# Layer 0 attention of a two-layer diffusion backbone: score tiles kept in PSUM, a bank for the context outputs, half heads ended later, dense bias tables

## The chip, the cores and the metric

The kernel runs on one core of one Trainium2 chip. The metric is device time in microseconds: the median over the runs of one kernel. All arithmetic is on fp32 data; each matmul operand is split into a high part in the matmul's own format (fp32r) and a low rest, so that most products take three matmuls (high x high, high x low, low x high).

## The reference, cut to what matters

1024 latent tokens on a 16 x 64 grid and 256 context tokens, width 1024, go through two layers. Layer 0 mixes by 16 heads of 64: eight neighbourhood heads (0 to 7), each query over a window of 8 rows by 16 columns and over the context, and eight grouped-query heads (8 to 15) over all 1280 tokens.

```python
# neighbourhood head: bias per (row offset, column offset), window scores and context scores in one softmax
col_bias = rpb[:, :, col_idx - cols[:, None] + (WIN_C - 1)]
s_win = einsum('bhqd,bhrqjd->bhrqj', q_r, k_win) * scale + bias
s_ctx = einsum('bhqd,bhkd->bhqk', q_r, kc) * scale
p = softmax(concatenate([s_win, s_ctx]))
# context tokens attend among themselves, in all 16 heads
yc_na, yc_g = grouped_attention(cnq, cnk, cnv), grouped_attention(cgq, cgk, cgv)
# six modulation vectors a layer
m = silu(cond) @ ada_w[l] + ada_b[l]
```

Then come the output projection, a SwiGLU layer, and layer 1 with differential attention, which the change leaves alone.

## The kernel before

All loads, and nearly all stores, are issued from SyncE's queue (SPq in the profile). The program is written in an order of its own and a scheduler of the framework places the instructions on the engines' queues by priority; within one tag the tiles of a pool go round a fixed number of buffers in the program's order. `later()` lowers the priority of what is written inside it by 3000, `tc.high_priority` raises it.

**Projections of layer 0** (to some 405 us). The value projection goes in two groups `g`, then chunks `ch` 0 to 7 give the neighbourhood heads' queries (0 to 3) and keys (4 to 7). Four things are slipped in between:

- `ada_acc` loads a modulation weight in eight tiles of 512 KB (tag `aw`, 3 buffers) and accumulates them on VectorE for two conditions (L210, L214); `ada_sum` adds the columns up with 16 small matmuls for each condition (L235) into a PSUM tile of tag `q`, 3 buffers here. Modulation 2 is loaded before the value projection, 3 at group 1, 4 at chunk 1, all under `later()`; the sums stand at group 1, chunk 1 and chunk 4.
- `tables(i, h)` builds the bias tables of a pair of heads for both orientations: a row of 15 x 127 values is broadcast into 64 partitions (L630), the column mask is added on GpSimd (L631) and the result is stored to DRAM (L634), in two tiles of tag `aw` with four loads and four stores in all. There are eight such calls, two in each value group and one in each of chunks 0 to 3. `skew` later reads each row at its own offset, so that row c of a table is shifted by c: 64 values at a time.
- `early` runs the first steps of `maxima`: for each head a score matmul without the split (L432) into a `q` tile and a row maximum on VectorE (L410; L406 with the bias). The largest value of each query is later taken off the scores by a 65th row of the key operand. 200 steps are asked for by the end of chunk 7, `EARLY0`; the rest (`side0`) run beside attention, done before head `NEWH` = 2.
- The operands of the first heads are loaded.

**Attention of layer 0** (474 to 913 us), heads 8 to 15, then 0 to 7. A head has one unit of the context tokens among themselves (256 queries, two key chunks side by side) and two halves of 512 queries: 10 key chunks each for a grouped-query head (21 units), 2 context chunks and 5 window units for a neighbourhood head (15 units). A unit is: two matmuls into a score tile `pst` (L853, L854); for a window unit the bias added by VectorE into an SBUF tile `sb` (L877); the exponential on ScalarE into `sb` (L843); the high part `hi`, on VectorE in one unit of three and on ScalarE otherwise (L846, L848); the low part `lo` = e - hi, on VectorE in one of four and on GpSimd otherwise (L849). Some units later three matmuls with the values follow (`pv_one`, L888 to L891), `LAG0` = 5 units behind, `LAGN` = 7 from head 2 on, where the flag `wide` is set. `finish` ends a half: logarithm and exponential of the sums (L901, L902) and three VectorE instructions (L903 to L905).

PSUM has eight banks: 3 `t` for scores, 3 `q` for maxima (from head 2 on also for every second score tile), 2 `v` for the outputs. At the end of each head all pending products run:

```python
            while pend:
                pv_one()
```

Of the kernel before, what the change touches and what calls it, by code (L numbers as in the profile page):

```python
# [9 lines left out]
F32 = mybir.dt.float32  # L10
# [7 lines left out]
P = 128  # L18
# [8 lines left out]
RPW = 127  # L27
RPN = 15 * RPW
# [4 lines left out]
LEADP, EARLY0, VSHARE, HIDVE, LAG0, PLHN = 0.9, 200, 0.3, 3, 5, 2  # L33
QB, VB, TB, X0, LOD = 3, 2, 3, 9, 4
# [18 lines left out]
def kernel(ctx: ExitStack, tc: tile.TileContext, xT, cond, ada_w, ada_b, win0, wv0, wout0, rp, rpf, qg, kg,  # L53
# [5 lines left out]
    def nm(s):  # L59
        uid[0] += 1  # L60
        return f"{s}_{uid[0]}"
# [55 lines left out]
    def dram(shape, name):  # L117
        return dpool.tile(shape, F32, name=name)
# [13 lines left out]
    sk = [dram([8, 64 * RPN + 2048], f"sk{i}") for i in range(2)]  # L132
# [18 lines left out]
    def skew(i, h, dr0, n):  # L151
        o = 63 + dr0 * RPW
        v = sk[i][h, o : o + 64 * (RPN - 1)].rearrange("(c n) -> c n", c=64)
        return v[:, : n * RPW].rearrange("c (u y) -> c u y", y=RPW)[:, :, :GW]

# [3 lines left out]
    def ps(tag, bufs, w=512):  # L159
        return pq[0].tile([P, w], F32, tag=tag, bufs=bufs, name=nm("ps" + tag))  # L160
# [137 lines left out]
    def later():  # L298

        return tc.high_priority(-LATER)  # L300
# [184 lines left out]
    with sbuf("hp0", 8) as hp, sbuf("a10", 8) as ap:  # L485
# [134 lines left out]
        cmt = ap.tile([P, 2, RPW], F32, tag="cmt", bufs=1, name="cmt")  # L620

        def tables(i, h):

            for d0, d1 in ((0, 8), (8, 15)):
                n = d1 - d0
                T = ap.tile([P, 8, RPW], F32, tag="aw", bufs=3, name=nm("sk"))[:, 0:n, :]
                T2 = T.rearrange("p u y -> p (u y)")
                for j in range(2):
                    src = (rpf, rp)[i][h + j : h + j + 1, d0 * RPW : d1 * RPW].to_broadcast([64, n * RPW])
                    nc.sync.dma_start(T2[64 * j : 64 * j + 64], src)  # L630
                nc.gpsimd.tensor_add(T, T, cmt[:, i : i + 1, :].to_broadcast([P, n, RPW]))  # L631
                for j in range(2):
                    dst = sk[i][h + j, : 64 * RPN].rearrange("(c n) -> c n", c=64)[:, d0 * RPW : d1 * RPW]
                    nc.sync.dma_start(dst, T2[64 * j : 64 * j + 64])  # L634

# [79 lines left out]
        for ch in range(8):  # L715
# [13 lines left out]
            if ch in (1, 4):  # L729
                ada_sum(*pend_ada, qmt)  # L730
            if ch == 1:
                with later():
                    pend_ada = ada_acc(ap, *adas.pop(0))
# [7 lines left out]
    with sbuf("a20") as ap, psum("pa20") as pq[0]:  # L741
# [4 lines left out]
        def stt_():  # L746

            turn[0] += 1
            return qmt() if wide and turn[0] % 2 else ps("t", TB)
# [106 lines left out]
        def attend(h):  # L856
# [11 lines left out]
            def unit(o, pieces, b=None):  # L868
# [3 lines left out]
                e = half()[:, :tot]  # L872
# [7 lines left out]
                hi, lo = probs(pst[:, :tot] if pieces[0][4] is None else e, tot, e)  # L880
# [4 lines left out]
            def pv_one():  # L885
# [6 lines left out]
                if done:  # L892
                    done()
# [14 lines left out]
            unit(pvt(), [(kc, 0, 256, 0, None) for kc in range(2)], 0)  # L908
# [12 lines left out]
            while pend:  # L921
                pv_one()

        pend = []
# [547 lines left out]
```

## Time and profile before

| | us |
|---|---|
| median of 3 runs | 3656.18 (3655.86 to 3661.64) |
| profiled execution, its time | 3658.97 |
| its span in the profile | 3657.2 |
| TensorE busy | 3415.5 (93%) |
| VectorE busy | 2218.4 (61%) |
| ScalarE busy | 1422.3 (39%) |
| GpSimd busy | 825.2 (23%) |

The span is the profiled execution from its first to its last instruction. Busy times are modelled for matmuls: each is shown until its result is out, so two in a row overlap, and the distance of their starts says what one costs.

### The profile page before, as it was taken

The numbers are of one execution on the slowest core, as the hardware profiler recorded it, in microseconds if no ns is written. First come the engines' busy times: TensorE is split into PE (matmuls) and PEld (weight loads), VectorE is DVE, ScalarE is ACT, GpSimd is POOL, SyncE is SP. The second block draws the span as 40 slices with busy tenths as digits, with TensorE's granted clock in tenths as the row PEclk, the third lists the DMA queues.
The fourth block names the chain that finished last, engine by engine and source line by source line (L and its number), as shares of the span: only waits on it lengthen the run. The fifth ranks groups of instructions, "written<-read, shape, count | busy, mean of one in ns | idle before, by whom it ended". The sixth has DMA issues, their size and how long they took to land.

```text
span 3657.2 us, 43706 instructions
## 1 busy us (share of the span) xinstructions
PE 3415.5 (93%) x16044; PEld 2783.9 (76%) x16044; DVE 2218.4 (61%) x3555; ACT 1422.3 (39%) x2862; POOL 825.2 (23%) x622
## 2 busy tenths in 40 slices
PE   6799699988999999999998899899999999999997
PEld 4588577766888888888886678787666888888886
DVE  7767388887755555554336366787998533433335
ACT  4431067666441111111115254797777421111112
POOL 3212177766220000000003322002332200000002
PEclk8899789999999999999999999999999999999999
DMA  5276764374413333231112553646442211111111
GB/s 212 78 241 223 219 136 103 87 142 97 165 52 98 104 104 98 93 98 47 35 41 87 135 140 100 201 149 189 125 127 91 98 47 50 49 53 47 47 47 64
DMA packets 198081, 394.51 MB, mean 108 GB/s; under 512 B 57692, under 2 KB 99216, under 8 KB 197866
## 3 DMA queue, kind: packets, MB, share of 16 engines
q1 hardware_dynamic: 196074, 388.62, 36.0%
q0 software_dynamic: 1792, 3.10, 0.2%
q8 instruction: 126, 2.06, 0.2%
q14 instruction: 89, 0.73, 0.1%
HBM read 317.03 MB, written 74.61 MB: 107 GB/s over the span
## 4 chain that ended last, share of the span: by engine, by line
PE 74%; DVE 10%; ACT 5%; POOL 3%; issue 3%; DMA 3%; SPq 1%; POOLq 0%; DVEq 0%; ACTq 0%
PE psd L181 6%; PE psd L182 6%; PE psd L183 6%; PE psg L181 5%; PE psg L182 5%; PE psg L183 5%; PE psu L183 4%; PE psu L181 4%; PE psu L182 4%; PE psm L183 4%; PE psm L182 4%; PE psm L181 4%; PE pst L1318 2%; PE psq L1063 2%; PE pst L1319 2%
## 5 line engine op out<-in xcount | busy, mean ns | idle before, releaser
L173 POOL TENSOR_TENSOR wl<-wr,wh 128x1024 fp32r<-128x1024 f32 x69 | 168.0, 2435 | 1521.7 <-ACT wh L172 1315.4
L172 ACT CAST wh<-wr 128x1024 fp32r<-128x1024 f32 x193 | 202.2, 1049 | 761.7 <-PE psd L182 305.7
L993 DVE SCALAR_TENSOR_TENSOR x<-psd,mods,x 128x512 f32<-128x512 f32 (+1 forms) x448 | 301.3, 686 | 190.7 <-PE psd L183 190.4
L1027 DVE TENSOR_TENSOR sg<-sg,psu 128x512 f32<-128x512 f32 (+1 forms) x110 | 69.6, 634 | 484.4 <-PE psu L183 477.9
L181 PE MATMUL psd<-ah,wh 128*128 128x512 f32 (+1 forms) x896 | 331.3, 370 | 8.8 <-DVE x L993 6.8
L182 PE MATMUL psd<-al,wh 128*128 128x512 f32 (+1 forms) x896 | 328.3, 366 | 0.0
L183 PE MATMUL psd<-ah,wl 128*128 128x512 f32 (+1 forms) x896 | 326.9, 366 | 0.8 <-DVE wl L173 0.7
L181 PE MATMUL psg<-hh,wh 128*128 128x512 f32 (+1 forms) x880 | 326.2, 371 | 0.9 <-ACT sg L1024 0.9
L183 PE MATMUL psg<-hh,wl 128*128 128x512 f32 (+1 forms) x880 | 325.3, 370 | 0.1
L182 PE MATMUL psg<-hl,wh 128*128 128x512 f32 (+1 forms) x880 | 325.0, 369 | 0.0
L183 PE MATMUL psu<-hh,wl 128*128 128x512 f32 (+1 forms) x880 | 323.8, 368 | 0.5 <-POOL wl L173 0.5
L181 PE MATMUL psu<-hh,wh 128*128 128x512 f32 (+1 forms) x880 | 324.1, 368 | 0.0
L182 PE MATMUL psu<-hl,wh 128*128 128x512 f32 (+1 forms) x880 | 323.6, 368 | 0.0
L173 DVE TENSOR_TENSOR wl<-wr,wh 128x1024 fp32r<-128x1024 f32 x124 | 156.0, 1258 | 220.7 <-ACT wh L172 204.8
L1065 DVE TENSOR_REDUCE st<-psq 128x1 f32<-128x512 f32 (+1 forms) x384 | 219.4, 596 | 58.3 <-PE psq L1064 53.5
L1066 ACT ACTIVATE psq<-psq,st 128x512 f32<-128x512 f32 (+1 forms) x384 | 226.8, 594 | 65.0 <-DVE st L1065 61.3
L181 PE MATMUL psm<-hh,wh 128*128 128x512 f32 (+1 forms) x584 | 219.2, 376 | 25.7 <-ACT wh L172 18.4
L849 POOL TENSOR_TENSOR pl<-sb,ph 128x512 fp32r<-128x512 f32 (+1 forms) x144 | 203.5, 1420 | 91.9 <-ACT ph L848 60.2
L182 PE MATMUL psm<-hl,wh 128*128 128x512 f32 (+1 forms) x584 | 217.4, 373 | 6.5 <-DVE hl L349 4.7
L183 PE MATMUL psm<-hh,wl 128*128 128x512 f32 (+1 forms) x584 | 217.9, 373 | 3.7 <-POOL wl L173 3.7
L181 PEld LDWEIGHTS psd<-ah,wh 128*128 128x128 f32 x896 | 169.4, 189 | 44.0 <-DVE x L993 13.5
L1024 ACT ACTIVATE sg<-psg 128x512 f32<-128x512 f32 (+1 forms) x110 | 60.5, 552 | 344.4 <-PE psg L183 344.4
(276 smaller groups left out, 8331.2 us busy)
## 6 DMA issues: line engine op xcount, KB each, us to landing
aw<-in_ada_w SPq DMA_DIRECT2D x112, 512.0 KB
wr<-in_wg SPq DMA_DIRECT2D x44, 512.0 KB
wr<-in_wu SPq DMA_DIRECT2D x44, 512.0 KB
wr<-in_wd SPq DMA_DIRECT2D x44, 512.0 KB
k<-ks SPq DMA_DIRECT2D x32, 640.0 KB
wr<-in_wout SPq DMA_DIRECT2D x32, 512.0 KB
q<-qs SPq DMA_DIRECT2D x32, 512.0 KB
k<-ks SPq DMA_DIRECT2D x48, 320.0 KB
```

The source lines that it names most:

```text
L172: nc.scalar.copy(hi, raw)
L173: (eng or nc.gpsimd).tensor_sub(lo, raw, f(hi))
L181: nc.tensor.matmul(o, ah, bh, start=start, stop=False)
L182: nc.tensor.matmul(o, ah, bl, start=False, stop=False)
L183: nc.tensor.matmul(o, al, bh, start=False, stop=stop)
L849: (nc.vector if npb[0] % LOD == 0 else nc.gpsimd).tensor_sub(lo, e, f(hi))
L993: nc.vector.scalar_tensor_tensor(xv, pst, mods[:, l, ci, 40 + oc : 41 + oc], xv, op0=ALU.mult, op1=ALU.add)
L1063: nc.tensor.matmul(p1, q2[:, a * P : a * P + P], k2[:, k0 : k0 + kw], start=True, stop=False)
L1065: nc.vector.tensor_reduce(st[:, 0, a, j : j + 1], p1, axis=AX.X, op=ALU.max, negate=True)
L1066: after_table(nc.scalar.activation(p1, p1, AF.Exp, bias=st[:, 0, a, j : j + 1], accum_out=st[:, 1, a, j : j + 1]))
L1318: nc.tensor.matmul(o, ks[c][1][:, kk], qs[c][1][:, c0 : c0 + 512], start=True, stop=False)
L1319: nc.tensor.matmul(o, ks[c][0][:, kk], qs[c][0][:, c0 : c0 + 512], start=False, stop=True)
```

## The change

Host side: the bias tables come as dense arrays `tabT` and `tabQ`, already laid out row by row with the shift of `skew` in them (64 columns in place of 127), gathered from the same values; the masks are 64 wide. `tables` is one tile, one load, one GpSimd addition and one store per call (16 DMAs in all for 64), and `skew` reads straight rows.

The last modulation accumulation (modulation 4) is written without `later()`, and its sum goes from chunk 4 to chunk 6.

In attention: `keep` marks the units whose low part VectorE makes: one of four as before, and every second one once `wide` is set. Their exponential (and the bias sum before it) is written in place into the PSUM score tile and not into `sb`. The high part is made on VectorE in one unit of four, never in a kept one. The context unit's output has a bank of its own (tag `c`), `q` has 2 buffers in place of 3, and of the wide heads' score tiles two of five take a `q` bank. `finish` is called two products (`LATEF`) after a half's last, and pending products are carried over from one head to the next.

```diff
-LEADP, EARLY0, VSHARE, HIDVE, LAG0, PLHN = 0.9, 200, 0.3, 3, 5, 2
-QB, VB, TB, X0, LOD = 3, 2, 3, 9, 4
+LEADP, EARLY0, VSHARE, LAG0, PLHN = 0.9, 200, 0.3, 5, 2
+QB, VB, TB, X0, LATEF = 2, 2, 3, 9, 2
...
     def skew(i, h, dr0, n):
-        o = 63 + dr0 * RPW
-        v = sk[i][h, o : o + 64 * (RPN - 1)].rearrange("(c n) -> c n", c=64)
-        return v[:, : n * RPW].rearrange("c (u y) -> c u y", y=RPW)[:, :, :GW]
+        return sk[i][64 * h : 64 * h + 64, dr0 * GW : (dr0 + n) * GW].rearrange("c (u y) -> c u y", y=GW)
...
         def tables(i, h):
-            for d0, d1 in ((0, 8), (8, 15)):
-                n = d1 - d0
-                T = ap.tile([P, 8, RPW], F32, tag="aw", bufs=3, name=nm("sk"))[:, 0:n, :]
-                T2 = T.rearrange("p u y -> p (u y)")
-                for j in range(2):
-                    src = (rpf, rp)[i][h + j : h + j + 1, d0 * RPW : d1 * RPW].to_broadcast([64, n * RPW])
-                    nc.sync.dma_start(T2[64 * j : 64 * j + 64], src)
-                nc.gpsimd.tensor_add(T, T, cmt[:, i : i + 1, :].to_broadcast([P, n, RPW]))
-                for j in range(2):
-                    dst = sk[i][h + j, : 64 * RPN].rearrange("(c n) -> c n", c=64)[:, d0 * RPW : d1 * RPW]
-                    nc.sync.dma_start(dst, T2[64 * j : 64 * j + 64])
+            T = ap.tile([P, 15, GW], F32, tag="aw", bufs=3, name=nm("sk"))
+            r = slice(64 * h, 64 * h + P)
+            nc.sync.dma_start(T.rearrange("p u y -> p (u y)"), (tabT, tabQ)[i][r])
+            nc.gpsimd.tensor_add(T, T, cmt[:, i : i + 1, :].to_broadcast([P, 15, GW]))
+            nc.sync.dma_start(sk[i][r], T.rearrange("p u y -> p (u y)"))
...
-            if ch in (1, 4):
+            if ch in (1, 6):
                 ada_sum(*pend_ada, qmt)
             if ch == 1:
-                with later():
-                    pend_ada = ada_acc(ap, *adas.pop(0))
+                pend_ada = ada_acc(ap, *adas.pop(0))
...
-            return qmt() if wide and turn[0] % 2 else ps("t", TB)
+            return qmt() if wide and turn[0] % 5 in (1, 3) else ps("t", TB)
...
-        def probs(src, w, e):
-            lo, hi = spare.pop() if spare else plh_more() if npb[0] % PLHN == 1 else plh()
+        def probs(src, w, e, keep):
+            lo, hi = spare.pop() if spare else plh_more() if npb[0] % PLHN == 0 else plh()
             lo, hi = lo[:, :w], hi[:, :w]
             after_table(nc.scalar.activation(e, src, AF.Exp))
-            npb[0] += 1
-            if npb[0] % HIDVE == 0:
+            if npb[0] % 4 == 2:
                 nc.vector.tensor_copy(hi, e)
             else:
                 nc.scalar.copy(hi, e)
-            (nc.vector if npb[0] % LOD == 0 else nc.gpsimd).tensor_sub(lo, e, f(hi))
+            (nc.vector if keep else nc.gpsimd).tensor_sub(lo, e, f(hi))
...
-                e = half()[:, :tot]
+                npb[0] += 1
+                keep = npb[0] % 2 == 1 if wide else npb[0] % 4 == 3
+                e = pst[:, :tot] if keep else half()[:, :tot]
...
                 if done:
-                    done()
+                    ends.append([LATEF, done])
+                for x in ends:
+                    x[0] -= 1
+                while ends and ends[0][0] < 0:
+                    ends.pop(0)[1]()
...
-            unit(pvt(), [(kc, 0, 256, 0, None) for kc in range(2)], 0)
+            unit(ps("c", 1), [(kc, 0, 256, 0, None) for kc in range(2)], 0)
...
-            while pend:
+            while pend and h == HEADS0[-1]:
                 pv_one()
+            while ends and h == HEADS0[-1]:
+                ends.pop(0)[1]()
```

## Rows read from the trace of the kernel before

**Rows 1.** Windows: stretch and length, busy (count) per engine, granted clock, DMA.
```profile
234.00:405.00 171.00, 166.19 (x883) 144.56 (x882) 101.02 (x191) 28.98 (x79) 41.15 (x22) 0.93 0.70 219
405.00:474.00 69.00, 32.65 (x88) 21.64 (x87) 45.18 (x71) 1.12 (x3) 11.59 (x15) 0.53 0.72 211
474.00:728.00 254.00, 242.47 (x1120) 191.60 (x1118) 216.19 (x414) 185.83 (x341) 194.24 (x160) 0.99 0.46 100
728.00:913.00 185.00, 157.14 (x713) 117.55 (x713) 151.55 (x257) 126.72 (x246) 114.94 (x107) 0.96 0.60 122
```

**Rows 2.** Waits, 390 to 480 us: total, times, longest.
```profile
PE psq L235 <- DVE acc L214: 33.7, 1, 33.7
```

**Rows 3.** Timeline of SyncE's queue: start, length, what, count.
```profile
234.68 1.14 SPq L630 DMA_DIRECT2D sk<-in_rpf  x2
...
295.04 5.03 SPq L207 DMA_DIRECT2D aw<-in_ada_w  x3
...
322.92 3.83 SPq L630 DMA_DIRECT2D sk<-in_rpf  x4
...
413.95 2.00 SPq L634 DMA_DIRECT2D sk<-sk  x3
416.00 17.27 SPq L207 DMA_DIRECT2D aw<-in_ada_w  x8
```

**Rows 4.** Timeline of TensorE and VectorE around the sums of line 235.
```profile
326.87 1.95 PE L235 MATMUL psq<-cst,acc 128*128 128x1 f32 x16 [0.77 <-DVE acc L214]
...
404.93 0.39 PE L183 MATMUL psm<-hh,wl 128*128 128x512 f32 x1
...
423.22 16.92 DVE L214 SCALAR_TENSOR_TENSOR acc<-aw,cs,acc 128x1024 f32<-128x1024 f32 x14 [0.22 <-DMA aw<-in_ada_w]
...
439.01 3.57 PE L235 MATMUL psq<-cst,acc 128*128 128x1 f32 x16 [33.69 <-DVE acc L214]
...
474.25 0.41 PE L853 MATMUL pst<-t,t 128*128 128x256 f32 x1
```

**Rows 5.** Lines 432 (to 405 us) and 410 (405 to 475): ns min/median/max.
```profile
L432 PE MATMUL psq<-km,qm x142: 274/392/797, 196.3 to 366.0; 128*128 128x512 f32 x87, 128*128 128x256 f32 x55
...
L410 DVE TENSOR_REDUCE mx<-psq x48: 411/680/692, 443.3 to 474.8; 128x1 f32<-128x512 f32 x32, 128x1 f32<-128x256 f32 x16
```

**Rows 6.** TensorE's groups by form, 405 to 475 us: busy, mean ns, idle before.
```profile
L432 PE MATMUL psq<-km,qm 128*128 128x512 f32 x32 | 21.8, 773 | 0.4
L432 PE MATMUL psq<-km,qm 128*128 128x256 f32 x20 | 8.2, 430 | 0.0
L235 PE MATMUL psq<-cst,acc 128*128 128x1 f32 x32 | 7.0, 348 | 33.7 <-DVE acc L214 33.7
```

**Rows 7.** The chain that ended last: start, length, what (clock at full speed).
```profile
477.34 0.23 PE psq L432
```

**Rows 8.** Groups by form, 474 to 728 us, VectorE and ScalarE.
```profile
L849 DVE TENSOR_TENSOR plh<-sb,plh 128x512 fp32r<-128x512 f32 x42 | 45.9, 1093 | 0.6 <-ACT plh L848 0.2
...
L846 DVE CAST plh<-sb 128x512 fp32r<-128x512 f32 x28 | 23.3, 833 | 1.6 <-ACT sb L843 1.4
...
L848 ACT CAST plh<-sb 128x512 fp32r<-128x512 f32 x57 | 35.4, 621 | 2.3 <-DVE hl L905 0.5
```

**Rows 9.** Line 849 from 474 to 728 us: ns min/median/max.
```profile
L849 DVE TENSOR_TENSOR plh<-sb,plh x42: 674/972/1836, 481.0 to 718.0; 128x512 fp32r<-128x512 f32 x42
```

**Rows 10.** Tile pst over the whole span (layer 1's subtraction): ns min/median/max.
```profile
L1329 DVE TENSOR_TENSOR pl<-pst,ph x80: 676/683/693, 2516.7 to 2816.4; 128x512 fp32r<-128x512 f32 x80
```

**Rows 11.** Waits, 474 to 735 us.
```profile
ACT rc L901 <- PE psv L891: 31.2, 8, 4.3
```

**Rows 12.** Waits, 728 to 913 us.
```profile
ACT rc L901 <- PE psv L891: 18.4, 8, 3.9
...
PE psv L888 <- DVE rc L904: 8.2, 5, 2.6
...
PE pst L853 <- DVE sb L877: 4.7, 7, 1.8
```

More of the change, by code (lines that the diff above doesn't have):

```diff
@@ L26 @@
 GW = 64
-RPW = 127
-RPN = 15 * RPW
 NEG = -1e30
@@ L52, with kernel @@
 @with_exitstack
-def kernel(ctx: ExitStack, tc: tile.TileContext, xT, cond, ada_w, ada_b, win0, wv0, wout0, rp, rpf, qg, kg,
+def kernel(ctx: ExitStack, tc: tile.TileContext, xT, cond, ada_w, ada_b, win0, wv0, wout0, tabT, tabQ, qg, kg,
                        win1, wv1, wout1, wg, wu, wd, lamv, subln, fgain, cosT, sinT, consts, cmT, cmQ, out):
@@ L131 @@
     onesrow = dram([2, NT], "onesrow")
-    sk = [dram([8, 64 * RPN + 2048], f"sk{i}") for i in range(2)]
+    sk = [dram([8 * 64, 15 * GW], f"sk{i}") for i in range(2)]
     def small_operands():
@@ L619 @@
                 gqa_q(g, w1, w2, o, blk)
-        cmt = ap.tile([P, 2, RPW], F32, tag="cmt", bufs=1, name="cmt")
+        cmt = ap.tile([P, 2, GW], F32, tag="cmt", bufs=1, name="cmt")
         def tables(i, h):
-            for d0, d1 in ((0, 8), (8, 15)):
-                n = d1 - d0
-                T = ap.tile([P, 8, RPW], F32, tag="aw", bufs=3, name=nm("sk"))[:, 0:n, :]
-                T2 = T.rearrange("p u y -> p (u y)")
-                for j in range(2):
-                    src = (rpf, rp)[i][h + j : h + j + 1, d0 * RPW : d1 * RPW].to_broadcast([64, n * RPW])
-                    nc.sync.dma_start(T2[64 * j : 64 * j + 64], src)
-                nc.gpsimd.tensor_add(T, T, cmt[:, i : i + 1, :].to_broadcast([P, n, RPW]))
-                for j in range(2):
-                    dst = sk[i][h + j, : 64 * RPN].rearrange("(c n) -> c n", c=64)[:, d0 * RPW : d1 * RPW]
-                    nc.sync.dma_start(dst, T2[64 * j : 64 * j + 64])
+            T = ap.tile([P, 15, GW], F32, tag="aw", bufs=3, name=nm("sk"))
[3 more added lines that the diff above has]
+            nc.sync.dma_start(sk[i][r], T.rearrange("p u y -> p (u y)"))
         mpool = None
@@ L879, in unit @@
                     off += w
-                hi, lo = probs(pst[:, :tot] if pieces[0][4] is None else e, tot, e)
+                hi, lo = probs(pst[:, :tot] if pieces[0][4] is None else e, tot, e, keep)
                 pend.append((v, vsl, o, parts, hi, lo, None if b is None else lambda: finish(o, b)))
@@ L920, in attend @@
                     yield
-            while pend:
+            while pend and h == HEADS0[-1]:
                 pv_one()
-        pend = []
+            while ends and h == HEADS0[-1]:
+                ends.pop(0)[1]()
+        pend, ends = [], []
         knots = [(0, 0), (X0, sum(27 if h > 7 else 19 for h in HEADS0) - done0)]
@@ L1409 @@
     rp = np.pad(inp["na_rpb"][0], ((0, 0), (0, 0), (48, 48)))
+    x = GW - 1 - np.arange(GW)[:, None] + np.arange(GW)[None, :]
+    tabQ, tabT = (t[:, :, x].transpose(0, 2, 1, 3).reshape(8 * GW, 15 * GW) for t in (rp, rp[:, ::-1, ::-1]))
     qgain, kgain = inp["gqa_q_gain"][0], inp["gqa_k_gain"][0]
@@ L1425 @@
     inside = (c[None, :] >= start[:, None]) & (c[None, :] < start[:, None] + 16)
-    x = np.arange(RPW)
-    kc = np.clip(c[:, None] + x[None, :] - 63, 0, GW - 1)
-    mq = np.where(inside[c[:, None], kc], f32(0), f32(NEG)).astype(f32)
-    qc = np.clip(c[:, None] + x[None, :] - 63, 0, GW - 1)
-    mt = np.where(inside[qc, c[:, None]], f32(0), f32(NEG)).astype(f32)
-    cmT, cmQ = np.concatenate([mt, mt], axis=0), np.concatenate([mq, mq], axis=0)
+    mq = np.where(inside, f32(0), f32(NEG)).astype(f32)
+    cmT, cmQ = np.concatenate([mq.T, mq.T], axis=0), np.concatenate([mq, mq], axis=0)
     arrays = dict(
@@ L1441 @@
         wout0=chunks(inp["par_w_out"][0], np.arange(D)),
-        rp=rp.reshape(8, RPN), rpf=rp[:, ::-1, ::-1].reshape(8, RPN),
+        tabT=tabT, tabQ=tabQ,
         qg=np.stack([np.tile(qgain[0::2], 4), np.tile(qgain[1::2], 4)], axis=1),
```

## Prediction

> **What bounds the kernel now.** I began with the page's 40 slices, which show where TensorE is not full, and then read four stretches of layer 0 with the windows view [rows 1]. The reader is to see four different things there. From 234 to 405 us (the projections of layer 0) TensorE is full: 166 of 171 us. From 405 to 474 it is busy for 33 of 69 us at a mean granted clock of 0.53. From 474 to 728 (the eight grouped-query heads) it is busy for 242 of 254 us, so only 11.5 us of idle time are left. From 728 to 913 (mostly the neighbourhood heads) it idles for 27.9 of 185 us, and VectorE is busy for 152. The rest of the kernel, 913 to 3657 us, the change does not touch.
>
> The hole at 405 is one wait. In the list of waits TensorE stands 33.7 us before the column sums of line 235, for the accumulation of line 214 on VectorE [rows 2]. The timeline shows it: the last projection matmul starts at 404.93, the sums at 439.01, the first score matmul of attention at 474.25 [rows 4]. The accumulation is late because its eight loads are issued from 416.00 on [rows 3]. Before them in the three-buffer ring of tag `aw` stand four bias tables of two tiles each, issued from 322.92, whose last stores leave at 413.95 [rows 3].
>
> The 35 us after the hole come from the same sum. By the program, 200 steps of row maxima should lie under the projections. By 405 us, 142 maxima matmuls had run [rows 5]; with six first steps of heads, which hold no matmul, that is 148. `early` reaches 200 x (0.3 + 0.7 x 6400/10240) = 147.5, so 148, exactly at the end of chunk 4, where the sum takes a buffer of the `q` ring. So the maxima stop where the program puts that sum, and 52 matmuls follow it [rows 6], at half clock, ahead of the first score.
>
> **The change, part by part.**
>
> *The last accumulation and its sum.* It loses its low priority, and its sum goes from chunk 4 to chunk 6. Ahead of its loads stand the same four tables, but each is one tile with one load and one store, of 0.49 MB each, where it was two tiles with two loads and two stores each. Two tables of four tiles took from 234.68 to 295.04, 15 us a tile; four tables of eight tiles took from 322.92 to 416.00, 11.6 us a tile [rows 3]. With two tiles less the accumulation before it starts some 30 us earlier (265) and lasts its 28 us (295.04 to 322.92); then four tiles at 11.6 us give 339, and loading and adding takes 24 us (416.00 to 440.1), so 363. Chunk 6 ends about 14 us before 405, at 391. Even at 15 us a tile it would be 377. I therefore cost the wait at nothing: minus 33.8 us (405.2 to 439.0).
>
> *The maxima behind it.* 35.2 us (439.0 to 474.25) become work under and after the projections. What TensorE still pays is the same work at full clock: 32 matmuls of 512 columns at 0.23 us and 20 of 256 at half of that [rows 6, 7], 9.8 us, and twice 16 column sums at 1.95 us [rows 4], 3.9. That is 13.7, so minus 21.5. The cover is VectorE. It must take 16 accumulations (18.3 us) and 52 reductions (30 us: 32 at 0.68, 20 at 0.41) into a stretch in which it is busy for 101 of 171 us [rows 1, 4, 5]: 149, or 87%. It holds 85% in the next stretch, so there is room, but hardly any. If there were none, the maxima would stand behind the projections at VectorE's pace, 30 us in place of 13.7: plus 16. I take plus 5, nearer to nothing because the share is one VectorE already reaches. First part: -33.8 - 21.5 + 5 = -50, between -55 and -39.
>
> *Tiles that VectorE splits stay in PSUM.* For a kept tile the exponential is written in place and VectorE subtracts from PSUM. The subtraction from SBUF takes 1.093 us in the mean over 42 [rows 8], with a median of 0.972 and a maximum of 1.836 [rows 9]; layer 1's subtraction of the same width from PSUM takes 0.683, and never over 0.693 [rows 10]. In the grouped-query stretch the share on VectorE stays 1 in 4, so 42 x 0.41 = 17 us less of VectorE; its casts go from 1 in 3 to 1 in 4, 14 fewer at 0.83, 12 us less; ScalarE gets those, 14 x 0.62 = 9 us more on 186 of 254. That PSUM reads are no dearer is what the row says. [...]
>
> In the wide heads the share on VectorE rises from 1 in 4 to 1 in 2 and GpSimd's falls from 3 to 2 in 4. VectorE's balance there is about even: 3.75 more subtractions a head at 0.68, against 3.75 at 1.09 that become cheaper and one cast less.
>
> *Banks.* Before, three outputs of a head went round two `v` banks; TensorE waits 8.2 us for a bank that line 904 still reads [rows 12]. The context output now has its own bank; the bank comes from `q`, which has two left for maxima in place of three. Scores of the wide heads go round five banks, not six.
>
> *Half heads ended later, and tiles left pending across heads.* ScalarE now stands before line 901 until the last product of a head is out: 31.2 us in the grouped-query stretch [rows 11], 18.4 in the next [rows 12], both off TensorE's path, but they hold back the next head's exponentials. The finish now comes two products later, and the products of a head end run between the next head's scores.
>
> *What I take for attention.* In the grouped-query stretch 11.5 us of idle are all there is to win by waits; I take half, -6. Bounds: -11 if all goes, +12 if each of 42 kept tiles costs 0.3 us of waiting for its bank. In the neighbourhood stretch a head takes 23.1 us (185/8). TensorE needs 16 (7104 columns through five matmuls at 0.23 for 512); VectorE 18.9 (151.55/8). I take half of the way to a VectorE floor of some 18.3: 2.4 x 8 = -19. Bounds: 0 and -38.
>
> *Dense tables.* Reading them takes runs of 3 KB where it took pieces of 256 bytes, and the table adds are 8 where they were 16. No TensorE wait hangs on them apart from those above: 0.
>
> **Sum.** -50 - 6 - 19 = -75 on a span of 3657.2, so 3582; the profiled execution's time is 1.8 above its span, 3584; the median of the runs shown is 2.8 below that execution's time: **3581 us**.
>
> **Rivals.**
>
> *The tail of the maxima stays in the open.* VectorE is full under the projections, or the four table tiles go at 23 us each, as whole tables did; then the sum comes about 406 and 18 steps follow. Speaks for it: 87% of VectorE. Against: the same load is carried at 474. Price: 11 to 16 us over what I took, 3592 to 3597.
>
> *PSUM gives back the gain in attention.* A kept tile holds its bank for the score (0.46), the exponential and the cast (0.6 each) and the subtraction (0.68), about 2.4 us in place of 1.1. Three `t` banks at a pace of 254/168 = 1.5 us a unit come round every 4.5 us, so 2.1 us are left for its waits in ScalarE's and VectorE's queues. If these are used up, score matmuls wait: attention gives nothing in the second stretch and loses 12 us in the first, so 3657 - 50 + 12 = 3619, and 3616 on the median's scale.
>
> *Slower than before.* The same mechanism decides the whole when each of the 94 kept tiles costs TensorE over 0.53 us (50/94), which needs queue delays of about 2.6 us per kept tile in the first stretch and more in the second. At 1 us each: 3581 + 25 + 94 = 3700. Against it: bank waits of scores are 4.7 us in the whole neighbourhood stretch now [rows 12].
>
> *The change does nothing to the hole.* If the accumulation still ended at 440, only attention's 25 us would be won: 3631. Against it: the ring in front of it is halved.
>
> **How the numbers follow.** Forecast 0.70, with its own range of 3552 to 3608 (first part -55 to -43, attention -48 to 0); maxima in the open 0.13; PSUM gives it back 0.11; hole stays 0.03; slower 0.03. The range that leaves no more than 2 in 10 out is 3546 to 3620. Faster by over 0.2% (7 us, about what a measurement of this kernel can tell from no change): 0.95; the same 0.02; slower 0.03.
>
> **What would show it.** In the profile after, no wait of line 235 over 2 us near 405; some 190 maxima matmuls ahead of the first score, which starts at 415 to 425; granted clock at full speed there. VectorE's line 849 reads `pst` at 0.68 us. The waits of line 888 for line 904 are gone, and a neighbourhood head takes 20 to 21 us. I am wrong if scores (line 853) wait for line 849, if maxima wait longer for their two banks, or if the sum still stands alone between projections and attention.

## The result and the profile after

The changed kernel takes 3610.18 us (median of 4 runs, 3604.61 to 3612.62) where the kernel before took 3658.68 beside it (4 runs): a ratio of 0.9865, 95% interval 0.9848 to 0.9882. That is 48.5 us less; 75 were predicted. The profiled execution took 3608.63 us, its span is 3606.8.

Three starting points cut the stretch that the change touches: the first score matmul, the first score of head 0 (the first neighbourhood head, eight heads later), and the last product of attention. They are read from the TensorE instructions of each trace. All kernels of this study by these points, in us; each ratio is against runs of the kernel before taken beside that kernel, whose median lay between 3658.68 and 3661.57:

| kernel | first score at | grouped-query heads | neighbourhood heads | median | ratio, 95% interval |
|---|---|---|---|---|---|
| before | 474.3 | 246.8 | 191.2 | 3658.68 | |
| the change | 435.2 | 238.8 | 190.9 | 3610.18 | 0.9865 (0.9848 to 0.9882) |
| a_tables | 427.9 | 249.3 | 190.8 | 3610.05, one run | |
| a_ada | 448.1 | 274.0 | 190.4 | 3654.11, one run | |
| a_both | 433.4 | 248.2 | 190.8 | 3615.17 | 0.9874 (0.9861 to 0.9888) |
| b_attn | 476.6 | 237.0 | 197.2 | 3662.14 | 1.0000 (0.9991 to 1.0009) |
| tables_attn | 427.7 | 239.8 | 190.1 | 3603.09 | 0.9843 (0.9829 to 0.9856) |
| keep_quarter | 436.2 | 242.7 | 193.3 | 3611.26 | 0.9871 (0.9856 to 0.9886) |
| keep_sbuf | 434.7 | 242.0 | 196.8 | 3616.91 | 0.9882 (0.9869 to 0.9896) |
| no_late | 434.6 | 242.3 | 183.9 | 3604.64 | 0.9849 (0.9835 to 0.9862) |
| early150 | 412.9 | 255.5 | 189.5 | 3601.83 | 0.9842 (0.9828 to 0.9855) |
| combo | 428.2 | 240.7 | 184.2 | 3598.29 | 0.9831 (0.9818 to 0.9845) |
| combo_hi | 430.1 | 238.6 | 177.2 | 3590.30 | 0.9807 (0.9794 to 0.9820) |
| combo_vec | 430.5 | 238.6 | 180.2 | 3591.61 | 0.9813 (0.9800 to 0.9826) |

The stages of a row come from one profiled execution, so small differences between them say little. tables_attn, combo, combo_hi and combo_vec are the same program up to the first score, and it starts at 427.7 to 430.5; the change, tables_attn and keep_quarter have the same grouped-query heads, and these take 238.8 to 242.7. So 3 or 4 us in one of these two stages are no finding by themselves. The neighbourhood heads agree better, 190.4 to 191.2 in the four kernels with the old attention.

The second row against the first is the result: 39.1 us are won ahead of the first score, 8.0 in the grouped-query heads, 0.3 in the neighbourhood heads; together 47.4. The rest of the kernel starts and ends that much earlier, and the span's other 3 us lie in work that the change doesn't touch.

The windows of the changed kernel, columns as in [rows 1], and behind them the neighbourhood heads of the kernel before, from their first score on:

```profile
234.00:405.00 171.00, 158.56 (x822) 135.82 (x821) 133.57 (x228) 27.94 (x77) 38.44 (x25) 0.91 0.60 208
405.00:435.00 30.00, 28.15 (x151) 23.16 (x149) 16.81 (x35) 2.40 (x5) 1.31 (x3) 1.00 0.76 203
435.00:674.00 239.00, 230.22 (x1072) 185.04 (x1073) 183.87 (x387) 193.48 (x347) 171.55 (x157) 0.99 0.42 104
674.00:865.00 191.00, 166.24 (x762) 130.32 (x760) 147.02 (x280) 137.47 (x269) 88.12 (x89) 0.93 0.57 134
...
721.00:912.00 191.00, 162.93 (x745) 122.01 (x744) 156.85 (x265) 130.27 (x252) 118.50 (x109) 0.96 0.61 128
```

The 69 us from 405 at a granted clock of 0.53 are now 30 us at full clock. But TensorE is less busy before them: 158.6 of 171 us where it was 166.2. In the neighbourhood heads VectorE falls from 82% of its window to 77%, GpSimd from 62% to 46%, and yet TensorE isn't full (87%), and its granted clock is lower, 0.93 for 0.96.

SyncE's queue after the change (line 623 loads a table, 625 stores it, 204 loads a modulation tile); the rows of before are [rows 3]:

```profile
298.87 0.33 SPq L623 DMA_DIRECT2D sk<-in_tabT  x1
...
316.36 0.33 SPq L623 DMA_DIRECT2D sk<-in_tabQ  x1
320.32 0.33 SPq L204 DMA_DIRECT2D aw<-in_ada_w  x1
324.04 2.52 SPq L625 DMA_DIRECT2D sk<-sk  x2
333.23 1.28 SPq L204 DMA_DIRECT2D aw<-in_ada_w  x3
```

Four tables pass in about 21 us, from 298.87 to the next modulation load at 320.32; before, the four took 93 (322.92 to 416.00). VectorE's and TensorE's timelines, for [rows 4]:

```profile
338.27 9.65 DVE L211 SCALAR_TENSOR_TENSOR acc<-aw,cs,acc 128x1024 f32<-128x1024 f32 x8
347.83 0.68 DVE L407 TENSOR_REDUCE mx<-psq 128x1 f32<-128x512 f32 x1
348.44 4.86 DVE L211 SCALAR_TENSOR_TENSOR acc<-aw,cs,acc 128x1024 f32<-128x1024 f32 x4
354.00 2.48 DVE L211 SCALAR_TENSOR_TENSOR acc<-aw,cs,acc 128x1024 f32<-128x1024 f32 x2 [0.71 <-DMA aw<-in_ada_w]
```

```profile
356.87 0.38 PE L429 MATMUL psq<-km,qm 128*128 128x256 f32 x1 [3.90 <-DVE mx L407]
...
412.88 1.84 PE L232 MATMUL psq<-cst,acc 128*128 128x1 f32 x16
...
430.11 0.40 PE L180 MATMUL psm<-hh,wl 128*128 128x512 f32 x1
...
435.17 0.63 PE L842 MATMUL pst<-t,t 128*128 128x256 f32 x2 [1.27 <-DVE t L354]
```

The sums (line 232, once 235) start at 412.88 without a wait, between projection matmuls: the hole is gone. But now 14 accumulations stand nearly back to back in VectorE's order with one reduction let through between them, and at 356.87 a maximum's matmul has waited 3.90 us, and every projection matmul behind it in TensorE's order with it (none starts between 352.68 and 358.66). The last projection starts at 430.11 where it started at 404.93.

The waits from 674 to 865 us, helpers first (columns as in [rows 2]):

```profile
POOL plh L838 <- DVE plh L835: 49.9, 26, 4.6
POOL plh L838 <- ACT plh L837: 33.0, 19, 4.1
...
PE psv L882 <- POOL plh L838: 7.1, 10, 1.1
PE psv L879 <- DVE rc L899: 5.1, 7, 2.3
PE psq L842 <- DVE pl L838: 3.9, 2, 2.2
...
PE pst L842 <- DVE pl L838: 2.3, 4, 1.0
```

The wait of the first product (line 879, once 888) for the end of a half head (899, once 904) is still there, 5.1 us for 8.2 [rows 12]. GpSimd stands 49.9 us before its subtraction, for a cast that VectorE has not made yet; then TensorE waits 7.1 us for that subtraction.

TensorE's time in the neighbourhood heads can be split by the starts of its matmuls: what they need at full clock (by their columns), what the stretches of low clock add, and the rest, waits. It is an estimate, good to 2 us (the sum runs to the next matmul after the stage):

| | matmuls at full clock | low clock | waits |
|---|---|---|---|
| before | 133.9 | 6.0 | 53.3 |
| the change | 137.3 | 11.6 | 44.1 |
| keep_sbuf | 137.3 | 10.0 | 51.7 |
| b_attn | 137.3 | 9.9 | 52.4 |
| no_late | 137.3 | 7.1 | 41.4 |
| combo | 137.3 | 7.1 | 41.8 |
| combo_hi | 137.4 | 2.9 | 38.9 |
| combo_vec | 137.4 | 1.6 | 43.7 |

The 3.4 us more of matmuls are five products of the head before that now run behind the first score of head 0 (15 of 0.23 us). So by this estimate the change takes 9.2 us of waits out of this stage, and loses them again: 3.4 to these products, 5.6 to the clock.

### The profile page after: what moved, and what is told of

It is laid out like the page before. It is cut to its first block, busy times and chain, and to the rows that moved or that the text cites. A ratio compares the mean times of both kernels' runs of the same rounds, so it can differ in the third digit from the quotient of the medians.

```text
span 3606.8 us, 43570 instructions
## 1 busy us (share of the span) xinstructions
PE 3395.8 (94%) x16044; PEld 2780.6 (77%) x16044; DVE 2185.3 (61%) x3553; ACT 1440.7 (40%) x2886; POOL 762.7 (21%) x592
## 4 chain that ended last, share of the span: by engine, by line
PE 76%; DVE 10%; ACT 6%; issue 3%; DMA 3%; POOL 2%; SPq 1%; POOLq 0%; DVEq 0%; ACTq 0%
PE psd L178 6%; PE psd L179 6%; PE psd L180 6%; PE psg L178 5%; PE psg L179 5%; PE psg L180 5%; PE psu L180 5%; PE psu L178 5%; PE psu L179 5%; PE psm L180 4%; PE psm L179 4%; PE psm L178 4%; PE pst L1315 2%; PE pst L1316 2%; PE psq L1060 2%
## 5 line engine op out<-in xcount | busy, mean ns | idle before, releaser
L990 DVE SCALAR_TENSOR_TENSOR x<-psd,mods,x 128x512 f32<-128x512 f32 (+1 forms) x448 | 301.2, 686 | 191.3 <-PE psd L180 191.2
L838 POOL TENSOR_TENSOR plh<-sb,plh 128x512 fp32r<-128x512 f32 (+2 forms) x144 | 183.3, 1277 | 140.4 <-DVE plh L835 64.0
```

Of the source, the lines that this page charges most:

```text
L838: (nc.vector if keep else nc.gpsimd).tensor_sub(lo, e, f(hi))
L990: nc.vector.scalar_tensor_tensor(xv, pst, mods[:, l, ci, 40 + oc : 41 + oc], xv, op0=ALU.mult, op1=ALU.add)
```

## Experiments on the part ahead of the first score

**a_tables**: the kernel before with the dense tables alone (`tables`, `skew`, and the arrays that feed them); accumulation and sum stay where they were.

```diff
-            for d0, d1 in ((0, 8), (8, 15)):
...
+            T = ap.tile([P, 15, GW], F32, tag="aw", bufs=3, name=nm("sk"))
+            nc.sync.dma_start(T.rearrange("p u y -> p (u y)"), (tabT, tabQ)[i][r])
```

> The kernel before with the dense tables alone: the last accumulation still has low priority and its sum still stands at chunk 4. Theory (the ring of four tables in front of the loads made them late): with half the tiles and bytes the loads come some 60 us earlier, the sum is ready before the projections end, the hole goes and the first score comes at 430 to 440. Rival (the low priority makes it late): the hole of 34 us stays and the first score comes at 465 to 475.

3610.05 us in one run. The first score starts at 427.9, 46.4 us earlier than before, 7.3 earlier than with the whole change, and ahead of the theory's 430 to 440.

```profile
298.20 0.33 SPq L624 DMA_DIRECT2D sk<-in_tabT  x1
...
318.65 0.33 SPq L205 DMA_DIRECT2D aw<-in_ada_w  x1
...
338.64 12.27 SPq L205 DMA_DIRECT2D aw<-in_ada_w  x4
...
360.57 3.87 SPq L205 DMA_DIRECT2D aw<-in_ada_w  x2
```

At low priority the loads are still issued from 318.65 on: it was the tables' time in the ring that made them late, not their priority. The accumulations come more spread out, and TensorE's waits from 234 us to the first score are shorter:

```profile
PE psq L233 <- DVE acc L212: 4.2, 3, 2.8
PE psq L430 <- DVE mx L408: 3.3, 5, 1.2
```

With the whole change the same two are longer:

```profile
PE psq L429 <- DVE mx L407: 7.4, 7, 3.9
PE psq L232 <- DVE acc L211: 5.3, 3, 3.7
```

**a_ada**: the kernel before with only the accumulation's normal priority and its sum at chunk 6.

```diff
-            if ch in (1, 4):
+            if ch in (1, 6):
...
-                with later():
-                    pend_ada = ada_acc(ap, *adas.pop(0))
+                pend_ada = ada_acc(ap, *adas.pop(0))
```

> The kernel before with the new place and priority of the last accumulation alone, tables as before. Theory: its loads still stand behind four tables of two tiles, which now are due earlier than before only if the scheduler lifts them, so the sum is still late, by 10 to 34 us; but 183 steps of maxima in place of 148 lie ahead of it, so that the first score comes at 440 to 465. Rival: priority alone lifts it past the tables, no hole, first score at 435.

3654.11 us in one run. The first score comes 26 us earlier (448.1, within the theory's 440 to 465) and the grouped-query heads take 27 us longer (274.0), so nothing is left by the end of these heads. SyncE's queue, and the waits from 440 to 520 us:

```profile
471.39 2.97 SPq L634 DMA_DIRECT2D sk<-sk  x4
474.41 1.92 SPq L783 DMA_DIRECT2D v<-vs  x2
```

```profile
DVE ph L845 <- PE psv L888: 25.1, 1, 25.1
...
PE pst L852 <- ACT sb L842: 13.8, 1, 13.8
...
PE psv L887 <- DMA v<-vs: 3.1, 1, 3.1
```

The slow tables now stand ahead of the loads of the first head's values (line 783), which TensorE's products need: the hole has moved into attention. So the new place and priority do nothing without short tables.

**a_both**: both edits on the kernel before, nothing in attention.

> The kernel before with the dense tables and the new place and priority of the last accumulation; attention as before. Theory: the two parts of the change add up, so this gives what the first score's start shows, 39 us: first score near 435 us, time near 3619. Rival: attention's own part is worth more than the 8 us the two traces show, and this gives only 25 to 30 us.

0.9874: all but 3 us of the change's gain by the ratios, whose intervals overlap; by the spans of the two profiled executions the rest is worth 7 us. The first score at 433.4 is the theory's 435. It is the first part that pays, and within it a_tables alone is no slower (3610.05 against 3615.17; one run against a median of four).

**early150**: the changed kernel with fewer maxima under the projections.

```diff
-LEADP, EARLY0, VSHARE, LAG0, PLHN = 0.9, 200, 0.3, 5, 2
+LEADP, EARLY0, VSHARE, LAG0, PLHN = 0.9, 150, 0.3, 5, 2
```

> The changed kernel with 150 steps of row maxima under the projections in place of 200. Theory: the first part gave 39 us and not 50 since maxima among the projection's matmuls make TensorE wait, in its order, for VectorE's reductions behind the accumulation. Then the 13.6 us of waits of maxima matmuls ahead of 436 us fall under 4, the last projection starts at 415 to 420 and the first score by 425; of that, some 10 us are given back where the 50 steps now run in attention: within 5 us of the changed kernel. Rival: VectorE's work up to the sum is the limit whatever the order, or the waits come from the accumulation's loads; then the last projection stays near 430 and the whole is 10 us slower.

The first score starts at 412.9, 22.3 us earlier, and TensorE's waits for line 407 up to there fall from 7.4 to 3.5 us:

```profile
PE psq L429 <- DVE mx L407: 3.5, 5, 1.3
```

The windows from 300 us to the last projection, of the changed kernel and then of early150:

```profile
300.00:430.00 130.00, 123.55 (x626) 104.27 (x626) 92.19 (x153) 13.39 (x25) 26.27 (x21) 0.95 0.56 187
300.00:409.00 109.00, 105.65 (x554) 88.60 (x554) 69.71 (x116) 11.35 (x22) 21.66 (x19) 0.98 0.64 213
```

The granted clock is 0.98 where it was 0.95.

The 48 maxima that are put off cost 16.7 us in the grouped-query heads. So one costs 0.46 us of TensorE's time under the projections (22.3/48) and 0.35 in attention (16.7/48). Of the 22.3 us some 9 are the columns of these maxima themselves (an estimate from their columns at full clock); the other 13 are waits and low clock, which the run doesn't separate. At 0.9842 the kernel is some 8 us below the changed one, though the intervals overlap a little. The theory's direction held: these waits fell under 4 us, the first score came earlier than it said, more was given back in attention than the 10 us that it expected, and the whole gained 8 us where it said within 5.

## Experiments on attention

**b_attn**: the kernel before with the attention part alone (everything from `stt_` to the end of the head loop, and the constants).

> The kernel before with attention's part alone (kept tiles, bank of the context output, late ends, products carried over heads). Theory: first score at 474 us as before, first score to the first sum of the output projection 443 us in place of 450.5: 6 to 10 us faster in all. Rival: attention's part is worth nothing or costs time by itself and only looks good behind an early start, 0 to -5 us.

1.0000, interval 0.9991 to 1.0009, over 11 runs: by itself the attention part is worth nothing, as the rival said. The grouped-query heads gain 9.8 us, the neighbourhood heads lose 6.0 and the first score comes 2.3 us later. Those 6.0 are, by the table above, the 3.4 of shifted products and 4 us more of low clock; the waits stay what they were (52.4 for 53.3). With dense tables the same edits give 190.1 (tables_attn), while the old attention takes the same time with either tables (191.2 before, 190.8 in a_tables). The largest wait of TensorE in b_attn's neighbourhood heads is that of the first product for the end of a half head; the changed kernel has 5.1 us of it. Why it is longer with the old tables stays open.

```profile
PE psv L889 <- DVE rc L909: 9.0, 8, 2.6
```

**tables_attn**: the whole change with the accumulation put back (a_ada's edit reversed).

> The changed kernel with the last accumulation put back (low priority, sum at chunk 4). Theory (the dense tables alone clear the hole, and the new place of the accumulation costs some 5 us of maxima waiting behind it): first score near 428 us and 3600 to 3606 us, no slower than the changed kernel. Rival (the new place is needed, the single look at the tables alone was lucky): 3612 or more.

0.9843 against 0.9865. The first score starts at 427.7, as in a_tables, and the median of 3603.09 is within the theory's 3600 to 3606. By the first scores (433.4 to 436.2 in the five kernels with the new place and dense tables at 200 maxima, 427.7 to 430.5 in the five without) the new place and priority cost some 6 us; the intervals of the ratios overlap.

**keep_sbuf**: the changed kernel, but the exponential of a kept tile is written to SBUF, as before.

```diff
-                e = pst[:, :tot] if keep else half()[:, :tot]
+                e = half()[:, :tot]
```

> The changed kernel with the same share of subtractions on VectorE, but their exponentials written into SBUF as before, so that no score bank is held. Theory (banks are what the kept tiles cost): scores no longer wait for the subtraction, waits of line 842 fall by 8 us or more in the last stretch, but the subtraction takes 1.0 to 1.1 us again; in all within 4 us of the changed kernel. Rival (the gain of a subtraction from PSUM is what attention lives on): attention 10 us or more longer.

Slower than the change by 3.2 us in the grouped-query heads, 5.9 in the neighbourhood heads, and 6 by the ratios, whose intervals overlap: between what the theory and the rival said. VectorE's subtraction by form in the grouped-query heads, here and then in the changed kernel:

```profile
L838 DVE TENSOR_TENSOR pl<-sb,ph 128x512 fp32r<-128x512 f32 x43 | 40.6, 944 | 2.1 <-ACT ph L837 1.6
```

```profile
L838 DVE TENSOR_TENSOR pl<-pst,ph 128x512 fp32r<-128x512 f32 x43 | 29.4, 684 | 1.9 <-ACT ph L837 1.6
```

From PSUM it takes 684 ns, as the prediction took from layer 1 [rows 10]. In the neighbourhood heads the waits are 51.7 us for 44.1, nearly those of before. So most of the waits that the change takes out of this stage (7.6 of 9.2 us) hang on this edit. The theory's saving did not come: the waits of scores for kept tiles (3.9 and 2.3 us with the change) are gone, but scores now wait 6.5 us in all for ScalarE's and VectorE's other steps, where they waited 7.5 us in all with the change.

**keep_quarter**: the changed kernel with VectorE's share in the wide heads at 1 in 4 again, as before.

```diff
-                keep = npb[0] % 2 == 1 if wide else npb[0] % 4 == 3
+                keep = npb[0] % 4 == 3
```

> The changed kernel with one kept tile in four in the wide heads too (before: every second); GpSimd gets the subtractions back. Theory (in the wide heads kept tiles hold banks and put VectorE into the chain from exponential to product): a neighbourhood head from the third on takes 23.0 to 23.4 us in place of 23.85, 3 to 6 us faster in all, fewer waits of scores for line 849's successor. Rival (GpSimd was what products waited for): a head takes over 24 us and the kernel is 3 to 8 us slower.

0.9871 against 0.9865: no difference that can be told, so neither theory nor rival came. (Its row in the table of stages is of a profiled execution 8.6 us above its median, and is not used.)

**no_late**: the changed kernel with half heads ended right behind their last product.

```diff
-QB, VB, TB, X0, LATEF = 2, 2, 3, 9, 2
+QB, VB, TB, X0, LATEF = 2, 2, 3, 9, 0
```

> The changed kernel with a half ended right after its last product. Theory (ScalarE's stand before the logarithm is off the path): the stand comes back in part, heads take the same time within 0.3 us, time within 4 us of the changed kernel. Rival (late ends are what shortens the grouped-query heads from 31.0 to 30.2 us): these heads take 31 us again, 6 us slower.

Neither expectation came: the kernel is not the same and not slower, it is faster. The neighbourhood heads take 183.9 us in place of 190.9. The wait of line 879 for line 899, 5.1 us with the change, is in none of TensorE's waits there:

```profile
PE psv L882 <- POOL plh L838: 5.6, 11, 0.7
PE psv L879 <- DVE plh L835: 4.2, 4, 2.0
PE psq L842 <- DVE pl L838: 2.0, 4, 0.8
```

Ending halves later holds one of the two `v` banks longer, and in a neighbourhood head the next half to use it comes after only seven units. Of the 7.0 us, 2.7 are waits and 4.5 the clock (11.6 to 7.1 by the split above; 0.95 granted over the stage for 0.93). In the grouped-query heads the late end seems to give 3.5 us here, but such stages differ by as much without cause; combo against tables_attn shows 0.9 there, and again 5.9 lost in the neighbourhood heads. By the ratios (0.9849 against 0.9865) it is 6 us, with overlapping intervals.

**combo**: tables_attn and no_late together.

> The changed kernel with two of its edits taken back: the last accumulation has its low priority and its sum at chunk 4 again, and a half head is ended right behind its last product. Each alone measured 0.9843 and 0.9849 of the kernel before, against 0.9865 for all of the change. If the two losses are independent (7 us at the maxima under the projections, 5 us in attention), they add: about 0.983, 3595 us. Rival: the end of the half heads only shifts which unit waits, and its 5 us were scatter: 0.984 to 0.9845, 3601 us.

0.9831, 3598.29 us: the number of the first theory. Its interval reaches into the rival's 0.984 to 0.9845; but the stages have both gains, the first score at 428.2 and the neighbourhood heads at 184.2 us.

**combo_hi**: combo, and VectorE casts no high part in the wide heads.

```diff
-            if npb[0] % 4 == 2:
+            if npb[0] % 4 == 2 and not wide:
```

> The kernel above, and in the wide heads every high part is cast by ScalarE (VectorE casts none there). Theory: a neighbourhood head's pace is set by a chain from engine to engine, in which GpSimd's subtraction stands 50 us behind a cast that waits in VectorE's order; with some 23 casts fewer there, that wait goes, and a head takes 0.5 to 1 us less: 4 to 8 us in all, 3590 us. Rival: ScalarE has the casts on top of exponentials and ends of half heads (133 of 177 us busy, plus 14 us), it becomes the late one and GpSimd waits for it instead: no gain, or 3 to 5 us slower.

0.9807, 3590.30 us, the fastest of all: 8 us below combo, 7.0 of them in the neighbourhood heads. Combo's window there, its GpSimd waits, and then the same of combo_hi:

```profile
669.00:853.00 184.00, 162.56 (x760) 125.81 (x760) 145.74 (x280) 137.23 (x269) 90.42 (x90) 0.95 0.59 139
```

```profile
POOL plh L840 <- DVE plh L837: 47.3, 26, 6.5
POOL plh L840 <- ACT plh L839: 30.9, 17, 3.8
```

```profile
669.00:846.00 177.00, 156.96 (x760) 122.50 (x758) 135.73 (x257) 146.15 (x286) 89.07 (x90) 0.98 0.61 145
```

```profile
POOL plh L840 <- ACT plh L839: 68.3, 38, 5.2
...
PE psq L844 <- DVE pl L840: 6.8, 9, 1.0
...
POOL plh L840 <- DVE plh L837: 4.8, 6, 1.8
```

The size came as the theory said, the way only in part. GpSimd's wait for VectorE's casts is gone but for 4.8 us, but its waits for ScalarE's grow: 73.1 us in all where it was 78.2, with a longest wait of 5.2 for 6.5 us. TensorE's own waits for high parts from VectorE (4.2 us in combo) are gone and those for GpSimd's subtractions shrink, while its scores wait longer for the banks of kept tiles: 8.5 us, 3.8 in combo. By the split above TensorE's waits fall by 2.9 us and low clock by 4.2: the granted clock is 0.98 for 0.95. The rival's bound did not come: ScalarE is at 146 of 177 us.

**combo_vec**: combo_hi, and every unit of the wide heads is kept, so GpSimd subtracts nothing there.

```diff
-                keep = npb[0] % 2 == 1 if wide else npb[0] % 4 == 3
+                keep = True if wide else npb[0] % 4 == 3
```

> As the kernel above, and in the wide heads every unit is kept: biases are added and exponentials are taken in PSUM, VectorE subtracts all low parts, and GpSimd none. Theory of the chain: the step to the engine that is late last (GpSimd's subtraction, up to 4.9 us behind its cast) is gone, VectorE has 47 subtractions at 0.7 us more and 23 casts at 0.9 fewer, some 150 of 177 us: a head takes 1 to 2 us less, 8 to 16 us in all, 3585 us. Rival, the floor that the prediction reckoned with: VectorE's load sets the pace, and with 12 us more of it the stage is longer by as much; or each bank is held longer and score matmuls wait for VectorE's subtraction: 3610 to 3620 us.

0.9813, the same as combo_hi; neither theory's number came. (The profiled execution took 3598.15 us, 6.5 above its median; 4.7 of its difference to combo_hi's lie behind attention.) The window and the largest wait of ScalarE:

```profile
669.00:849.00 180.00, 161.69 (x760) 120.93 (x759) 159.84 (x302) 142.63 (x284) 35.34 (x45) 0.99 0.60 142
```

```profile
ACT pst L835 <- DVE pst L870: 27.5, 14, 3.2
```

VectorE has 24 us more to do than in combo_hi (159.8 against 135.7) and the stage is 3.0 us longer. So its load alone is not what the pace goes by. With GpSimd out of the chain another link is late: the longest wait of ScalarE is now that of the exponential for VectorE's bias add, and TensorE's waits rise by 4.8 us.

## Why the prediction was off, step by step

3610 us lies inside the range of 3546 to 3620, and 2 us outside the forecast's own range of 3552 to 3608. (By the parts named for it, -43 and 0, that range would have ended at 3613; and 3619 on the span is 3618 on the median's scale, not 3616.) The direction was right, and the hole, which brings most of the gain, went as forecast; two terms were mis-sized, the maxima and above all the neighbourhood heads.

**The last accumulation and its sum: right in effect, wrong in its reason.** Minus 33.8 us was reckoned for the hole, and no wait is left at this sum. The accumulation was expected to end about 363; the last row above ends at 356.5. That it is so near is partly luck: the four tables took 21 us and not 46, and loading and adding behind them 36 us and not 24. And the prediction moved the sum and shortened the ring together and never priced one alone. a_tables shows that the shorter tables in the ring do it all, and a_ada that the move alone does nothing.

**The maxima behind the projections: the term that failed in the first part.** 13.7 us of work and 5 of tail were allowed from the last projection of before (404.9) to the first score, 18.7. It took 30.3 (to 435.2), so the first part gave 39.1 and not 50. I had asked whether VectorE has room, and it has: 133.6 of 171 us, where 149 were reckoned. Much of the cost lies in order, not in load: a maximum's matmul that waits for a bank (3.90 us at 356.87) stops the projection matmuls behind it, and a_tables and tables_attn, with the same maxima and accumulations in another order, have the first score 7 us earlier. From 200 us to the first score TensorE's matmuls need 196 us at full clock in both kernels (summed from their columns, an estimate). On top of this, waits other than the hole's 33.8 cost 12 us up to the last projection before, and cost 26 up to the first score now; low clock cost 10 us there and costs 13 now. The rival "the tail stays in the open" had almost this price (11 to 16 us over what I took; measured 11.6), but not this place: 185 of the 194 maxima run before the last projection and 9 behind it. About 7 of the 11.6 are the new place and priority (tables_attn, a_tables); the rest, some 4 us, is not taken apart by any run: early150, with fewer maxima, has both less waiting and less low clock. The prediction's sign of being wrong, that maxima wait longer for two banks in place of three, came (7.4 us), but not through the bank: from 200 us to the first score line 430 waits 6.9 us for reductions in a_both, which has three banks, and 3.5 in a_tables with three and in tables_attn with two.

**The subtraction from PSUM: right.** 0.684 us, with minimum and maximum 0.671 and 0.693 over 43, against a mean of 1.093 [rows 8]. From SBUF the slow cases are among those that overlap GpSimd's subtractions: of 64 subtractions of 512 columns on line 849 before, the 12 that overlap a GpSimd subtraction by at most a twentieth average 0.687 us and the 30 that lie wholly under one 1.164 (overlaps counted from the instruction records, in which GpSimd's spans are rough; 7 of the 30 take 0.674 to 0.678 us all the same). With one operand in PSUM there are no slow cases: of the 79 of this width in the changed kernel (line 838), the 22 that lie wholly under a GpSimd subtraction average 0.684 us, and the longest of them takes 0.692. So from PSUM it takes what it takes from SBUF without GpSimd, 0.684 and 0.687 us.

**Grouped-query heads: about right.** -6 was forecast, -8.0 measured, 3.4 of it the five products that now run in the next stage, so some 4.6 are left of it. Kernels with the old attention take 246.8 to 249.3 us here (a_ada apart), those with the new one and 200 maxima 237.0 to 242.7.

**Neighbourhood heads: the step that failed most.** -19 was taken, as half the way from 23.1 us a head to a VectorE floor of 18.3. It gave -0.3. The 23.1 was itself read from a window that begins 7 us behind the first score of head 0; from that score on a head took 23.9 (191.2/8) and VectorE was busy for 19.6 of it (156.85/8). VectorE's busy time did fall, by 9.8 us, and TensorE's waits by 9.2, not by 19. The step that failed is the floor: combo_vec has 24 us more VectorE work than combo_hi and takes 3 us more, so a head's time does not follow VectorE's load. What it follows is argued and only in part shown: a chain through four engines (score, bias, exponential, high part, low part, product), in which each step is late by its place in some engine's order. Then 3.4 us came in from the head before, and 5.6 went to the clock, a term that the prediction had for the first part and not for this one. The late end of half heads costs 7 us (no_late), and the high parts left to VectorE, all of them now for GpSimd's units, another 7 (combo_hi). I had priced the late end within a gain, since ScalarE stood 18.4 us before line 901 [rows 12], a wait that I had myself called off TensorE's path; the bank that a late end holds was on it. So my sign of success, no more waits of line 888 for 904, did not come either, nor a head of 20 to 21 us (191/8 is 24).

**Dense tables: nothing was reckoned for reading them.** With the old attention that holds (191.2 and 190.8 us in the neighbourhood heads); with the new one the stage is 7 us shorter with dense tables (197.2 and 190.1), which stays open.

**The rivals in attention.** "PSUM gives back the gain" named waits of scores for kept tiles. They exist, line 842 for line 838, 3.9 and 2.3 us in the neighbourhood heads, but they did not eat the gain: keep_sbuf, which frees the bank early, is not faster but some 6 us slower.

**What stays open.** Letting products stay pending across heads, and the separate bank of the context outputs, were not tried alone. Nor was early150 joined to combo_hi, which may be faster still. What share of the waits is owed to which link of the chain is open too.

## What to carry to other kernels

When a transfer is late, look first at what stands before it in its buffer ring and make that short; moving and promoting the late step alone only moved the hole here (a_ada: the first score 26 us earlier, the stage behind it 27 us longer). Work slipped between the matmuls of TensorE where it was full (166.2 of 171 us before) cost its waits as well as its columns, since what stood behind it in TensorE's order waited too (early150: 0.46 us a maximum, of which by the estimate above some 0.19 are columns). Where no engine is full, do not take an engine's busy time for the pace (combo_vec: 24 us more of VectorE's work, a stage 3 us longer): find the link that is late, take it out, and look for the next one, and check whether a postponed step holds a buffer that something on the path needs (no_late: the stage is 7 us shorter without the postponed end).

## What the runs showed that was not expected

Here the clock took back much of what the waits gave. In the neighbourhood heads before the change the waits were 53.3 us and low clock cost 6.0; with the change they are 44.1 and 11.6. In the changed kernel TensorE is granted half speed (0.50) in six stretches there, where it was three before: three of 3.4 us, two of 6.8 and one of 17.1 that reaches past the last product. These rows show the two of 6.8 us, each behind the 10 us before it, in which TensorE was busy for 7.7 and 7.2 us:

```profile
784.50:794.50 10.00, 7.74 (x37) 5.41 (x35) 5.11 (x11) 5.99 (x12) 3.57 (x5) 1.00 1.04 246
794.80:801.60 6.80, 6.54 (x17) 5.47 (x18) 4.52 (x10) 4.85 (x9) 1.47 (x3) 0.50 0.93 211
808.40:818.40 10.00, 7.22 (x32) 4.85 (x31) 4.42 (x8) 6.76 (x13) 4.71 (x7) 1.00 1.03 222
818.70:825.50 6.80, 6.28 (x20) 5.50 (x21) 4.89 (x9) 1.49 (x3) 1.00 (x1) 0.50 0.12 25
```

In no_late and combo_hi the waits are less still, 41.4 and 38.9 us, and low clock costs 7.1 and 2.9; so it has to be read beside the waits in each version. And the end of a half head is slow in the same cases as the subtraction: line 905 of the kernel before, SBUF to SBUF, takes 0.685 us free of GpSimd's subtractions (10 cases) and 1.419 in the mean when at least nine tenths of it lie under one (10 cases, three of them not slowed).
